# The joint output projection of a hybrid trunk layer: results kept in SBUF, norm and transposes at other places, and the order of five smaller steps

## The chip, the cores and the metric

The kernel runs on one core of one Trainium2 chip. The metric is device microseconds (us) of one execution; the time before is the median of three runs.

## The reference

One layer of a decoder, 2048 tokens of width 1024, all in float32:

```python
u    = rmsnorm(h, attn_pre_norm)
proj = u @ w_in                                     # 1024 -> 3584, split into:
hq, hf, hi, hg, sq, sk, sv = split(proj)            # 512 columns each
o_hg = rmsnorm(hgrn2_mix(hq, hf, hi), hg_out_norm) * silu(hg)   # recurrence, 4 heads of 128 x 128, chunks of 64
o_sb = rmsnorm(stick_breaking_mix(sq, sk, sv), sb_out_norm)     # causal attention, 8 heads of 64
mix  = concatenate([o_hg, o_sb]) @ w_out            # 1024 -> 1024
h    = h + rmsnorm(mix, attn_post_norm)
gate, up = split(rmsnorm(h, ffn_pre_norm) @ w_gate_up)          # 1024 -> 2 x 2816
h    = h + rmsnorm((silu(gate) * up) @ w_down, ffn_post_norm)
h    = h + (p @ ple_proj) * sigmoid(h @ ple_gate)
```

## The kernel before

The 2048 tokens are worked in four groups (0 to 3) of 512. A float32 operand is split into a high part, cast by ScalarE, and a low part, subtracted by VectorE or GpSimd (`split`, `w_prep`), and each product is three TensorE matmuls (`mm3`, L216 to L219: the lines of nearly all matmuls). A tile of 128 x 512 float32 has 256 KB. Results between the stages lie in HBM: `o_s` (raw results of recurrence and attention, eight tiles of each group, 0 to 3 of the recurrence and 4 to 7 of attention), `on_s` (the same normed), `un_s` (normed rows for the FFN), `u_s` (these rows transposed), `h_s` and `h2_s` (the residual stream).

TensorE's order is the program's order. The order of VectorE, ScalarE, GpSimd and SP (all DMAs are issued on SP's queue) is set by the framework's list scheduler from its own estimates, except for instructions put through `tc.keep_in_program_order`. Streams (Python generators) are laid between each other by `weave(main, slots, (stream, steps, phase), ...)`: so many slots of the main stream, with the steps of each other stream spread over them. A `Rate` gives a stream its share of steps per slot.

The stages in order of time:

- Input projection of the four groups (`in_proj`), with the attention (`att_stream`) and the recurrence (`hgrn`) woven in. `in_norm` norms the rows, `in_u` transposes them. The first projection's products use the PSUM banks of tag `mm`.
- `out_proj` of groups 0 and 1, 16 slots each. The rest of the attention is spread over 30 of the 32 slots (`2 * OP_SLOTS - 2`). In group 1's slots lie also `post_mix` of group 0 (`pm`: norm and residual, four tiles, written to `h_s` and `un_s`), the turn of these rows (`tu`), and `first_rows`, which prepares group 2's operands for the next stage.
- `out_pair`, the joint projection of groups 2 and 3 ("the pair"): seven block products in the order `CHAIN` (1, 2, 6, 3, 7, 5, 4), each of four steps of 12 matmuls. `w_prep` prepares the weights of the next product, `a_prep` its other operand; both come in the first two steps of a product. `scaled` multiplies a raw result by its row scales (`over_rows`) and stores it in `on_s`. `post_mix` and the turn of group 1 are woven in:

```python
weave(op, 2)
weave(op, 5, (pm, TT, 0))
weave(op, 5, (tu, 9, 0), (Stream(first_operands()), ND, 1))
```

- FFN (`gate_up`, `down`) and the gated embedding (`ple`), run by `Drive`. Its stage 0 begins with block products too, b0p1 and so on, whose operands are made by `t_first` (four tiles of a product) and `t_second`. Other work is hung on its steps by `at` and `spread`: `post_late` (norm and residual of groups 2 and 3) and `turner` (turn of these rows).

`turn` is used for all these transposes. It loads row tiles one pair of blocks ahead (`get`); for groups 2 and 3 ScalarE multiplies the loaded rows by `scales`. Then TensorE transposes four blocks of 128 x 128 into a bank, ScalarE evicts the bank into `e` and multiplies by the gain, and `e` is stored in `u_s`.

## Time and profile before

| | |
|---|---|
| median of three runs | 3021.26 us (3021.04 to 3026.05) |
| the profiled execution | 3015.62 us |
| its span | 3013.8 us |
| mean granted TensorE clock | 0.983 |
| TensorE busy | 2869.5 us |
| VectorE busy | 2105.5 us |
| ScalarE busy | 1575.3 us |
| GpSimd busy | 1425.1 us |

PE is TensorE's matmuls, PEld its weight loads, DVE is VectorE, ACT is ScalarE, POOL is GpSimd, and SPq is SP's queue of DMAs. A row of the waits such as `PE tr L914 <- DMA wr<-un_s: 21.8, 2, 13.8` reads: TensorE, about to write tile `tr` at line 914, waited for the DMA that fills `wr` from `un_s`; 21.8 us in all, 2 times, 13.8 us the longest. A row of the timeline gives the begin in us, the busy time of the group, the engine, line, operation, tiles and shapes, the count, and in brackets the idle time before it and what ended it. A row of the DMA list gives the count, the KB of each and the median us from issue to landing. The granted clock is the share of full speed that TensorE was given.

### The profile page before, as it was taken

The page shows a single profiled execution, that of the slowest core. Times are in us where ns is not written, and L with a number is a line of the kernel's source. Part 1 is how long each engine was busy: PE and PEld are TensorE (multiplying, and loading weights), DVE is VectorE, ACT ScalarE, POOL GpSimd, SP SyncE. Part 2 cuts the span into 40 slices and gives each one's busy share as a digit, 9 for nine tenths or more (in the row PEclk, how much of TensorE's full clock was granted, in tenths as well). Part 3 has the DMA queues.
Part 4 walks back from the last instruction along what each step waited for, and adds up shares of the span by engine and source line. Part 5 has one row for each costly group of instructions (what it writes and reads, how often), then busy time and mean ns, then how long its engine had stood idle before and what let it go on. Part 6 is the DMA issues. An engine that isn't in the chain of part 4 may idle for free. (4 is left out here: it accounts for less than half of the span.)

```text
span 3013.8 us, 51897 instructions
## 1 busy us (share of the span) xinstructions
PE 2869.5 (95%) x17772; PEld 2401.6 (80%) x17772; DVE 2105.5 (70%) x3035; ACT 1575.3 (52%) x3174; POOL 1425.1 (47%) x1412
## 2 busy tenths in 40 slices
PE   8899999999999999876889999999999999999999
PEld 7788788888887888865777777788888888888777
DVE  3766667687777777756877777755787766565685
ACT  5666766676767676754533334355533333445542
POOL 3344546555556667745443222255822121456653
PEclk9999999999999999987999999999999999999999
DMA  7975655565445454477876787777975555677975
GB/s 216 313 215 160 182 175 164 148 179 165 151 139 157 144 157 138 154 233 256 299 234 216 230 286 253 249 232 208 313 252 173 175 161 181 213 216 230 331 249 168
DMA packets 478712, 626.60 MB, mean 208 GB/s; under 512 B 44656, under 2 KB 270960, under 8 KB 478448
## 3 DMA queue, kind: packets, MB, share of 16 engines
q1 hardware_dynamic: 478448, 623.29, 65.8%
q8 instruction: 140, 2.29, 0.3%
q14 instruction: 124, 1.02, 0.1%
HBM read 455.88 MB, written 167.25 MB: 207 GB/s over the span
## 5 line engine op out<-in xcount | busy, mean ns | idle before, releaser
L980 POOL TENSOR_TENSOR wl<-wr,wh 128x512 fp32r<-128x512 f32 x256 | 375.2, 1473 | 437.4 <-ACT wh L979 390.3
L979 ACT CAST wh<-wr 128x512 fp32r<-128x512 f32 x600 | 350.7, 618 | 437.5 <-PE mm L218 91.2
L443 POOL TENSOR_TENSOR a<-be,ring 128x512 f32<-128x512 f32 (+2 forms) x320 | 321.7, 1005 | 405.2 <-DVE ring L439 372.8
L980 DVE TENSOR_TENSOR wl<-wr,wh 128x512 fp32r<-128x512 f32 x344 | 305.3, 895 | 179.2 <-ACT wh L979 154.5
L217 PE MATMUL mm<-uh,wh 128*128 128x512 f32 x992 | 412.1, 415 | 11.4 <-ACT uh L979 4.2
L219 PE MATMUL mm<-uh,wl 128*128 128x512 f32 x992 | 391.7, 395 | 6.2 <-DVE wl L980 6.1
L218 PE MATMUL mm<-ul,wh 128*128 128x512 f32 x992 | 391.3, 394 | 5.0 <-POOL ul L980 5.0
L439 DVE TENSOR_TENSOR_SCAN ring<-z,ring,be 128x512 f32<-128x512 f32 x192 | 245.6, 1279 | 95.1 <-ACT z L425 91.0
L217 PE MATMUL mm<-wh,uh 128*128 128x256 f32 (+1 forms) x856 | 266.7, 312 | 4.2 <-DVE vv L358 4.2
L218 PE MATMUL mm<-wl,uh 128*128 128x256 f32 (+1 forms) x856 | 252.6, 295 | 2.6 <-POOL wl L980 2.6
L219 PE MATMUL mm<-wh,ul 128*128 128x256 f32 (+1 forms) x856 | 252.2, 295 | 0.0
L217 PEld LDWEIGHTS mm<-uh,wh 128*128 128x128 f32 x992 | 188.5, 190 | 50.3 <-ACT uh L979 4.7
L219 PEld LDWEIGHTS mm<-uh,wl 128*128 128x128 f32 x992 | 188.1, 190 | 49.6 <-DVE wl L980 7.4
L456 DVE TENSOR_TENSOR al<-tr,ah 128x512 fp32r<-128x512 f32 (+1 forms) x320 | 191.7, 599 | 49.7 <-ACT ah L454 47.7
L424 ACT ACTIVATE be<-z 128x512 f32<-128x512 f32 (+2 forms) x320 | 171.1, 535 | 105.4 <-DVE z L422 65.9
L203 ACT CAST wh<-wr 128x512 fp32r<-128x512 f32 x256 | 158.7, 620 | 125.2 <-PE mm L218 65.2
L218 PEld LDWEIGHTS mm<-ul,wh 128*128 128x128 f32 x992 | 188.7, 190 | 37.2 <-POOL ul L980 5.5
L454 ACT CAST ah<-tr 128x512 fp32r<-128x512 f32 (+1 forms) x320 | 167.8, 524 | 81.2 <-PE tr L451 79.1
L204 POOL TENSOR_TENSOR wl<-wr,wh 128x512 fp32r<-128x512 f32 x128 | 168.6, 1317 | 81.7 <-ACT wh L203 75.3
L980 POOL TENSOR_TENSOR wl<-s,wh 128x512 fp32r<-128x512 f32 x44 | 67.9, 1547 | 259.2 <-ACT wh L979 232.5
L418 PE MATMUL z<-kt,q 128*128 128x512 f32 (+3 forms) x640 | 187.8, 374 | 0.0
L451 PE MATMUL tr<-ident,a 128*128 128x128 f32 x1088 | 175.8, 275 | 8.3 <-POOL a L443 8.0
(362 smaller groups left out, 7553.8 us busy)
## 6 DMA issues: line engine op xcount, KB each, us to landing
wr<-in_w_gate_up_dram SPq DMA_DIRECT2D x308, 256.0 KB, 4.0
wr<-in_w_in_dram SPq DMA_DIRECT2D x224, 256.0 KB, 3.2
wr<-hid_s SPq DMA_DIRECT2D x154, 256.0 KB, 3.3
wr<-in_w_down_dram SPq DMA_DIRECT2D x110, 256.0 KB, 3.8
wr<-h_s SPq DMA_DIRECT2D x96, 256.0 KB, 4.2
wr<-wd_s SPq DMA_DIRECT2D x88, 256.0 KB, 3.1
kt<-k_s SPq DMA_DIRECT2D x80, 256.0 KB, 3.2
vt<-v_s SPq DMA_DIRECT2D x80, 256.0 KB, 3.2
```

The lines of the kernel that those rows point to most:

```text
L204: (lo_engine or nc.gpsimd).tensor_tensor(lo, src, hi.bitcast(F32), op=ALU.subtract)
L217: nc.tensor.matmul(o, l[0], r[0], start=start, stop=False)
L218: nc.tensor.matmul(o, l[0], r[1], start=False, stop=False)
L219: nc.tensor.matmul(o, l[1], r[0], start=False, stop=stop)
L418: nc.tensor.matmul(z[:, :n], st["q"][i][:, tb * P:(tb + 1) * P], ch["k"][:, :n], start=i == 0, stop=i == 1)
L424: nc.scalar.activation(be[:, :n], z[:, :n], AF.Sigmoid, scale=0.125)
L439: nc.vector.tensor_tensor_scan(r[:, o:o + n][:, ::-1], z[:, :n][:, ::-1], be[:, :n][:, ::-1], init, op0=ALU.mult, op1=ALU.bypass)
L443: nc.gpsimd.tensor_tensor(a[:, :n], be[:, :n], r[:, o + 1:o + n + 1], op=ALU.mult)
L451: nc.tensor.transpose(tr[:, tb * P:(tb + 1) * P], ch["a"][tb][:, sb * P:(sb + 1) * P], ident)
L456: nc.vector.tensor_tensor(lo[:, lo_c:], tr[:, lo_c:], hi[:, lo_c:].bitcast(F32), op=ALU.subtract)
L979: nc.scalar.copy(hi, src)
L980: lo_engine.tensor_tensor(lo, src, hi.bitcast(F32), op=ALU.subtract)
```

## The change

Seven things are changed.

- First input projection: its products use two tags of banks (`mm`, `tr`: four banks) instead of one, and group 1's transposes use `z` in place of `tr`. The squares of `in_norm` for groups 2 and 3 are kept in program order.
- Attention is spread over 29 slots instead of 30 and drained after the thirteenth slot of group 1's projection. That projection is woven as 6 + 3 + 4 + 3 slots: `pm` of group 0 in the first 6, the turn from the tenth slot on. The last square of group 3's attention results is made there too, and both row scales of group 3 (`rr3`) are computed ahead of the pair.
- `out_pair` loads group 3's eight raw results into weight buffers (`wl`, `wh`, and two `wr`) and uses them from there; they are no longer stored in `on_s[3]` nor loaded from it. All are scaled at step 1 of the first product, where product 6's operands are made too, the low parts on VectorE. The weights of product 2 are prepared after these loads; the low parts of product 6's weights go to GpSimd.
- In the pair the norm of group 1 lies in slots 0 to 3, `first_operands` in slots 4 to 6, the turn in slots 7 to 11, and slot 12 holds the operands of the FFN's product 6 (`third_operands`), which were made in the FFN's first two steps.
- `t_second` of the FFN's first product goes one `k` to a step (steps 1 to 4) instead of two to a step (steps 2 and 3).
- In `turn` the multiplication by `scales` is taken out of the load and put behind the eviction of the second block, in program order.
- The turner of group 2 begins at step 34 instead of 36; both turners have one step more.

The diff; the changes of line numbers and of two signatures (`placed`, `rr`) are left out:

```diff
...
                     nc.vector.scalar_tensor_tensor(
                         shared, y, 1.0 / D, y, op0=ALU.mult, op1=ALU.mult, accum_out=ss[:, j:j + 1])
                 else:
-                    nc.scalar.activation(junk, y, AF.Square, scale=ROOT, accum_out=ss[:, j:j + 1])
+                    placed(nc.scalar.activation(junk, y, AF.Square, scale=ROOT, accum_out=ss[:, j:j + 1]))
         r = const.tile([P, 1], F32, tag="ssum", name="ssum", bufs=8)
         nc.gpsimd.tensor_scalar(r, ss[:, 0:1], ss[:, 1:2], EPS, op0=ALU.add, op1=ALU.add)
         if out is None:
...
             (nc.gpsimd if g == NG - 1 else nc.vector).tensor_tensor(raw, raw, r, op=ALU.mult)
         else:
             nc.vector.scalar_tensor_tensor(raw, raw, g_sb[:, i - HH:i - HH + 1], r, op0=ALU.mult, op1=ALU.mult)
-        nc.sync.dma_start(on_s[g][i], raw)
+        if g == NG - 2:
+            nc.sync.dma_start(on_s[g][i], raw)
 
     def first_rows(g, tt):
         acc = ev(name="oss")
...
                 if k % 2:
                     yield
 
-    def out_pair(g, tt, acc):
+    def out_pair(g, tt, rr):
         sw = {}
         cs = [{} for _ in range(TT)]
         raws, s2 = {}, {}
...
             else:
                 hi, lo = operand(wpool, "u", UB)
             nc.scalar.copy(hi, raw)
-            (V if k % 2 else G).tensor_tensor(lo, raw, hi.bitcast(F32), op=ALU.subtract)
+            (V if k % 2 and pos != 2 else G).tensor_tensor(lo, raw, hi.bitcast(F32), op=ALU.subtract)
             sw[prod, k] = hi, lo
 
         def a_prep(pos, k):
...
                 sub(V, s2[k], a12, s2[k])
                 t, e = s2[k], G
             elif prod == 7:
-                t, a21 = load(on_s[g][k]), load(on_s[g + 1][k])
-                sub(V, t, t, a21)
+                t = load(on_s[g][k])
+                sub(V, t, t, raws[k])
                 e = V
             elif prod == 5:
-                t, a22 = load(on_s[g + 1][k]), load(on_s[g + 1][HH + k])
-                add(V, t, t, a22)
+                t = raws[k]
+                add(V, t, t, raws[HH + k])
                 e = G
             else:
-                t, e = load(on_s[g + 1][HH + k]), V
+                t, e = raws[HH + k], V
             tt[prod, k] = split(wpool, "u", UB, t, e)
 
         def rows(half, j, i):
...
 
         def before(pos, i):
             if (pos, i) == (0, 1):
-                raws["r"] = [over_rows(row_scale(hgss[:, g + 1, :]), "tr", new_acc)]
+                raws["r"] = [over_rows(r, "tr", new_acc) for r in rr]
                 for k in range(HH):
                     scaled(g + 1, k, raws[k], raws["r"][0])
-            elif (pos, i) == (0, 3):
-                raws["ss"] = row_scale(tile_sums(acc))
-            elif (pos, i) == (1, 1):
-                raws["r"].append(over_rows(raws["ss"], "tr", new_acc))
                 for k in range(HH):
                     scaled(g + 1, HH + k, raws[HH + k], raws["r"][1])
                     t = load(on_s[g][k])
                     sub(V, t, raws[k], t)
                     add(V, t, t, raws[HH + k])
                     s2[k] = t
-                    tt[6, k] = split(wpool, "u", UB, t, G if k % 2 else V)
+                    tt[6, k] = split(wpool, "u", UB, t, V)
 
         def new_acc():
             return slot("acc", 0, "acc")
 
-        for pos in range(2):
-            for k in range(HH):
-                w_prep(pos, k)
-        for k in (*range(HH), *range(HH, ND)):
-            raws[k] = load(o_s[g + 1][k])
-        sq = new_acc()
-        nc.scalar.activation(sq, raws[ND - 1], AF.Square)
-        nc.gpsimd.tensor_tensor(acc, acc, sq, op=ALU.add)
+        for k in range(HH):
+            w_prep(0, k)
+        for i in range(ND):
+            if i in (2, 3):
+                raws[i] = slot("wr", 0, "wr")
+            else:
+                tag = "wh" if i % 2 else "wl"
+                raws[i] = wpool.tile([P, GT], F32, tag=tag, name=tag, bufs=3)
+            nc.sync.dma_start(raws[i], o_s[g + 1][i])
+        for k in range(HH):
+            w_prep(1, k)
         for pos, prod in enumerate(CHAIN):
             for i in range(TT):
                 before(pos, i)
...
                 r = new_in().rearrange("p (t d) -> p t d", t=2)
                 rows = src[2 * i * P:2 * (i + 1) * P, q * 256:(q + 1) * 256]
                 nc.sync.dma_start(r, rows.rearrange("(t p) d -> p t d", p=P))
-                for n in range(2):
-                    if scales:
-                        nc.scalar.activation(r[:, n, :], r[:, n, :], AF.Copy, scale=scales[2 * i + n])
-                    ts.append(r[:, n, :])
+                ts.extend((r[:, 0, :], r[:, 1, :]))
             return ts
+
+        def scale(ts):
+            if scales:
+                for t, r in zip(ts, scales):
+                    tc.keep_in_program_order(nc.scalar.activation(t, t, AF.Copy, scale=r))
 
         nxt = get(0)
         yield
+        if scales:
+            scale(nxt)
+            yield
         for q in range(4):
             ts = nxt
             nxt = get(q + 1) if q < 3 else None
...
                 else:
                     nc.scalar.activation(e, b, AF.Copy, scale=gain[:, k:k + 1])
                 nc.sync.dma_start(dst[k], e)
+                if nxt and c:
+                    scale(nxt)
                 yield
 
     def make_pt():
...
     for i in range(WARM):
         nc.tensor.transpose(warm[:, i % TT * P:(i % TT + 1) * P], ident, ident)
     Stream(in_u(in_norm(0), us[0], ["mm", "mm", "tr", "z", "z", "av", "tr", "hg"])).drain()
-    u1 = Stream(in_u(in_norm(1), us[1], ["z", "av", "tr", "hg"]))
+    u1 = Stream(in_u(in_norm(1), us[1], ["z", "av", "z", "hg"]))
     build_masks(nc, att, masks)
+    mm_tags[:] = ["mm", "tr"]
     main = Stream(in_proj(0, us[0], KQV))
     weave(main, ND // 2)
     later = tc.keep_in_program_order
...
     weave(main, ND, (u1, ND, 0))
     main.drain()
     u1.drain()
+    mm_tags[:] = ["mm"]
 
     units = [attention_steps(g) for g in range(NG)]
     res = [{} for _ in range(NG)]
...
             un.drain()
         main.drain()
     todo = total_units - spent + LAG + 2
-    rates = Rate(att_stream, 2, todo, 2 * OP_SLOTS - 2)
+    rates = Rate(att_stream, 2, todo, 2 * OP_SLOTS - 3)
     r2 = Rate(hgs[2], 1, HG_STEPS - 42, 2)
     r3 = Rate(hgs[3], 1, HG_STEPS, 2 * OP_SLOTS - 2)
     half = OP_SLOTS // 2
...
             weave(op, OP_SLOTS - 2, rates.part(OP_SLOTS - 2), r3.part(OP_SLOTS - 2))
         else:
             rows = Stream(first_rows(2, tto))
-            weave(op, half, rates.part(half), r3.part(half), (pm, TT, 0), (rows, 3, 1))
+            weave(op, 6, rates.part(6), r3.part(6), (pm, TT, 0), (rows, 3, 1))
+            weave(op, 3, rates.part(3), r3.part(3))
             tu = Stream(turn(un_s[0], u_s[0], g_ffn, ["tr"], xt, ev))
             acc3 = ev(name="oss")
             square_sums(acc3, 0, 3, range(HH - 1), xt)
-            weave(op, half, rates.part(half), r3.part(half), (tu, 9, 0), (rows, 6, 1))
+            weave(op, 4, rates.part(4), r3.part(4), (tu, 5, 0), (rows, 4, 1))
+            att_stream.drain()
+            square_sums(acc3, 0, 3, (HH - 1,), xt)
+            weave(op, 3, r3.part(3), (tu, 4, 0), (rows, 2, 1))
             hgs[3].drain()
-            att_stream.drain()
+            rr3 = [row_scale(hgss[:, 3, :]), row_scale(tile_sums(acc3))]
             rows.drain()
             side.close()
             big[0] = ctx.enter_context(tc.tile_pool(name="bigr", bufs=1, side="right"))
...
 
     drive = Drive([(gate_up(0, tt0), 3), (down(0), 4), (gate_up(1, tt1), 3), (down(1), 4),
                    (ple(0, ss0), 5), (ple(1, ss1), 5)])
-    op = Stream(out_pair(2, tto, acc3))
+    op = Stream(out_pair(2, tto, rr3))
     tu = Stream(turn(un_s[1], u_s[1], g_ffn, ["tr", "hg"], lambda: slot("wr", 0, "wr"), ev))
 
-    weave(op, 2)
-    weave(op, 5, (pm, TT, 0))
-    weave(op, 5, (tu, 9, 0), (Stream(first_operands()), ND, 1))
+    def third_operands():
+        for k in range(ND // 2):
+            t_first(0, tt0, 6, k)
+            yield
+
+    weave(op, 4, (pm, TT, 0))
+    weave(op, 3, (Stream(first_operands()), ND, 1))
+    weave(op, 5, (tu, 9, 0))
+    weave(op, 1, (Stream(third_operands()), ND // 2, 0))
     drive.prepare(2)
     op.drain()
     wpool_open.close()
...
         return turn(src, dst, gain, ["hg"], wr, acc, scales)
 
     for k in range(ND // 2):
-        at(0, k // 2, lambda k=k: t_first(0, tt0, 6, k))
-        at(0, 2 + k // 2, lambda k=k: t_second(0, tt0, k))
+        at(0, 1 + k, lambda k=k: t_second(0, tt0, k))
     spread(0, 6, post_late(NG - 2), 2 * TT, 3)
     spread(0, 19, post_late(NG - 1), 2 * TT, 4)
     for k in range(DFF // 256):
         at(0, 36 + 4 * k, lambda k=k: down_combos(k))
-    spread(0, 36, turner(h_s[2], u_s[2], g_ffn, rows_h[0]), 9, 2)
-    spread(0, 54, turner(h_s[3], u_s[3], g_ffn, rows_h[1]), 9, 2)
+    spread(0, 34, turner(h_s[2], u_s[2], g_ffn, rows_h[0]), 10, 2)
+    spread(0, 54, turner(h_s[3], u_s[3], g_ffn, rows_h[1]), 10, 2)
     spread(2, 59, make_pt(), 9, 2)
     for k in range(ND // 2):
         spread(1, 3 + 18 * k, t_all(1, tt1, k), 9, 2)
...
```

What the schedulers make of it, at three places.

VectorE in the pair, about the norm of group 1: `mix<-mix,rstd,gb` is the norm of a tile (the number tells the tile), `h<-h,mix` its residual, `cu` and `c_...` evictions of the pair's products, `ul<-wr,uh`, `wl<-wr,wh` low parts of operands. Before, the last two tiles:

```order
1447 L987 TENSOR_TENSOR c_18839<-z,cu 128x512
1448 L204 TENSOR_TENSOR ul<-wr,uh 128x512
1449 L864 SCALAR_TENSOR_TENSOR mix<-mix,rstd_18626,gb 128x512 x2
1450 L865 TENSOR_TENSOR h<-h,mix 128x512
1451 L864 SCALAR_TENSOR_TENSOR mix<-mix,rstd_18734,gb 128x512 x2
1452 L865 TENSOR_TENSOR h<-h,mix 128x512
1453 L980 TENSOR_TENSOR ul<-wr,uh 128x512 x2
1454 L987 TENSOR_TENSOR c_18900<-av,cu 128x512
```

And now, with the last tile:

```order
1445 L997 TENSOR_TENSOR cu<-av,cu 128x512
1446 L997 TENSOR_TENSOR cu<-mm,cu 128x512
1447 L778 TENSOR_TENSOR wl<-wr,wh 128x512
1448 L867 SCALAR_TENSOR_TENSOR mix<-mix,rstd_18613,gb 128x512 x2
1449 L990 TENSOR_TENSOR ul<-wr,uh 128x512
1450 L994 TENSOR_TENSOR wr<-wr,wl 128x512
1451 L994 TENSOR_TENSOR wr<-wr,wh 128x512
1452 L868 TENSOR_TENSOR h<-h,mix 128x512
1453 L997 TENSOR_TENSOR cu<-z,cu 128x512
```

The last tile's norm stood behind the third tile's at once; now two evictions and a low part of weights stand right ahead of it, and three other operations between it and its residual.

ScalarE in the FFN's stage 0, about a turner step: `acc<-hg` is the eviction of a transposed bank, `wr<-wr,row_scales` the scaling of loaded rows, `wh<-wr` casts of operands, `sg<-` the FFN's activation. Before:

```order
1904 L979 CAST wh<-wr 128x512 x4
1905 L919 ACTIVATE acc<-hg,g_ffn 128x512
1906 L979 CAST wh<-wr 128x512 x2
1907 L901 ACTIVATE wr<-wr,row_scales 128x256 x2
1908 L979 CAST wh<-wr 128x512
1909 L901 ACTIVATE wr<-wr,row_scales 128x256 x2
1910 L1164 ACTIVATE sg<-c_21541 128x512
1911 L919 ACTIVATE acc<-hg,g_ffn 128x512
```

And now:

```order
1905 L989 CAST wh<-wr 128x512 x4
1906 L927 ACTIVATE acc<-hg,g_ffn 128x512
1907 L989 CAST wh<-wr 128x512 x3
1908 L1174 ACTIVATE sg<-c_21502 128x512
1909 L927 ACTIVATE acc<-hg,g_ffn 128x512
1910 L908 ACTIVATE wr<-wr,row_scales 128x256 x4
1911 L989 CAST wh<-wr 128x512
```

The scaling of a load's rows stood between two evictions; now all four scalings stand behind the second eviction.

SP's queue of DMAs ahead of the pair: `o_s_7<-avo` stores the last attention result of group 3, `wr<-o_s_...` loads group 3's raw results, `un_s<-mix` stores normed rows of group 1, `wr<-wo_s` loads weights. Before:

```order
814 L866 DMA h_s_88<-h 128x512
815 L474 DMA o_s_7_152<-avo 64x512
816 L866 DMA h_s_88<-h 128x512
817 L964 DMA wr<-o_s_0_145 128x512
818 L964 DMA wr<-o_s_1_146 128x512
819 L964 DMA wr<-o_s_2_147 128x512
820 L964 DMA wr<-o_s_3_148 128x512
821 L964 DMA wr<-o_s_4_149 128x512
822 L964 DMA wr<-o_s_5_150 128x512
823 L964 DMA wr<-o_s_6_151 128x512
824 L964 DMA wr<-o_s_7_152 128x512
825 L870 DMA un_s_96<-mix 128x512 x2
```

And now, from the store of that result on (`xt<-o_s_7` is the load for its square, `xt<-un_s` loads rows of group 0 to be turned, `u_s<-ev` stores turned rows, `raw<-o_s` are loads of `first_rows`, `gb` and `h` loads of group 1's norm):

```order
804 L477 DMA o_s_7_152<-avo 64x512
805 L705 DMA xt<-o_s_7_152 128x512
806 L901 DMA xt<-un_s_95 128x2x256 x2
807 L928 DMA u_s_99<-ev 128x512 x2
808 L753 DMA raw<-o_s_6_143 128x512
809 L753 DMA raw<-o_s_7_144 128x512
810 L859 DMA gb<-in_attn_post_norm_dram 128x512 x2
```

The store stood just ahead of the eight loads of raw results; now the load for the last square follows it at once, and the loads into `wl` and `wh` come later (from row 813 on).

More of the change, by code (lines that the diff above doesn't have):

```diff
@@ L257, in dense_op, with row_rstd @@
             yield banks[i]
-    def row_rstd(halves, out=None, ss=None, shared=None):
+    def row_rstd(halves, out=None, ss=None, shared=None, placed=lambda ins: ins):
         if ss is None:
@@ L296, in in_norm @@
                     nc.sync.dma_start(halves[j], x[r0:r0 + P, j * GT:(j + 1) * GT])
-            r = row_rstd(halves, shared=att.tile([P, GT], F32, tag="be", name="sq") if g == 0 else None)
+            if g < 2:
+                r = row_rstd(halves, shared=att.tile([P, GT], F32, tag="be", name="sq") if g == 0 else None)
+            else:
+                r = row_rstd(halves, placed=tc.keep_in_program_order)
             for h in halves:
@@ L814, in before @@
                     s2[k] = t
-                    tt[6, k] = split(wpool, "u", UB, t, G if k % 2 else V)
+                    tt[6, k] = split(wpool, "u", UB, t, V)
         def new_acc():
             return slot("acc", 0, "acc")
-        for pos in range(2):
-            for k in range(HH):
-                w_prep(pos, k)
-        for k in (*range(HH), *range(HH, ND)):
-            raws[k] = load(o_s[g + 1][k])
-        sq = new_acc()
-        nc.scalar.activation(sq, raws[ND - 1], AF.Square)
-        nc.gpsimd.tensor_tensor(acc, acc, sq, op=ALU.add)
+        for k in range(HH):
[3 more added lines that the diff above has]
+                raws[i] = slot("wr", 0, "wr")
+            else:
+                tag = "wh" if i % 2 else "wl"
[3 more added lines that the diff above has]
+            w_prep(1, k)
         for pos, prod in enumerate(CHAIN):
```

## The prediction

> **What bounds the kernel now.** I read the page's slices first, then TensorE's waits, then the same stretches as windows, and last the timelines of the engines those waits name.
>
> ```profile
> span 3013.8 us, 51897 instructions
> PE 2869.5 (95%) x17772; PEld 2401.6 (80%) x17772; DVE 2105.5 (70%) x3035; ACT 1575.3 (52%) x3174; POOL 1425.1 (47%) x1412
> PE   8899999999999999876889999999999999999999
> PEclk9999999999999999987999999999999999999999
> ```
>
> TensorE is busy 95% of the span, so 3013.8 - 2869.5 = 144 us is all its idle time. Each digit is 75 us; the dip (7, 6, 8, 8 from slice 18 on) lies between 1280 and 1580 us, and there the granted clock drops too. Who ends the idle:
>
> ```profile
> PE tr L914 <- DMA wr<-un_s: 21.8, 2, 13.8
> PE hg L914 <- ACT acc L919: 11.6, 4, 3.7
> PE tr L914 <- DMA xt<-un_s: 8.3, 1, 8.3
> PE mm L219 <- DVE wl L980: 6.1, 1, 6.1
> PE tr L712 <- POOL oss L827: 5.4, 1, 5.4
> PE mm L218 <- POOL ul L980: 5.0, 1, 5.0
> PE mm L217 <- ACT uh L979: 4.2, 1, 4.2
> PE z L218 <- POOL ul L774: 3.1, 1, 3.1
> PE z L218 <- DVE ul L774: 1.9, 1, 1.9
> PE mm L217 <- ACT wh L979: 1.1, 1, 1.1
> PE mm L217 <- DVE vv L358: 4.6, 4, 1.5
> PE mm L217 <- DVE eb L344: 1.5, 2, 0.8
> ```
>
> Columns: total us, times, longest. The last two rows are those of the first 120 us. Windows (from:to, length, then busy time and count of PE, PEld, DVE, ACT and POOL, granted clock, DMA share, GB/s):
>
> ```profile
> 1205.60:1281.20 75.60, 67.67 (x720) 61.12 (x718) 57.64 (x86) 56.43 (x133) 57.46 (x70) 0.95 0.48 153
> 1290.10:1340.90 50.80, 45.17 (x488) 42.08 (x489) 31.93 (x49) 27.34 (x55) 25.01 (x24) 0.92 0.66 219
> 1339.00:1522.00 183.00, 133.80 (x561) 106.80 (x560) 130.46 (x168) 90.14 (x182) 94.14 (x80) 0.85 0.78 264
> 1424.00:1468.20 44.20, 43.73 (x207) 36.11 (x206) 32.96 (x45) 28.88 (x60) 24.11 (x26) 1.00 1.00 349
> 1468.20:1498.00 29.80, 29.24 (x129) 23.87 (x128) 27.67 (x43) 13.89 (x25) 8.58 (x7) 1.00 0.78 264
> 1523.00:1600.00 77.00, 77.00 (x341) 63.75 (x340) 58.42 (x82) 23.37 (x48) 27.02 (x22) 1.00 0.73 240
> 1700.00:1910.00 210.00, 198.40 (x889) 162.74 (x888) 153.94 (x229) 76.91 (x146) 46.00 (x33) 0.98 0.79 260
> ```
>
> The third, 1339 to 1522 us, is the joint projection of groups 2 and 3 ("the pair") and the start of the FFN up to the first rows of `post_late`: 49 us idle and a mean clock of 0.85. The change is aimed at this stretch and at four smaller places. I take them in order of time.
>
> **1. First input projection, four banks instead of two.** The `vv` and `eb` rows are TensorE waiting for a PSUM bank not yet evicted: 4.6 + 1.5 = 6.1 us. With four banks a whole group of products (48 matmuls of 77.00/341 = 0.226 us, 10.8 us) lies between two uses of a bank, against a longest wait of 1.5. The second group's transposes leave `tr` for `z`, so the banks do not collide. **-6.1** (0 to -6.1). The squares of `in_norm` for groups 2 and 3 are pinned to their place in ScalarE's order; no wait above names them: 0.
>
> **2. Turn of the first group's rows.** The 8.3 us wait is for the load of `un_s[0]`, whose last store comes just before it:
>
> ```profile
> 1282.73 0.94 SPq L870 DMA_DIRECT2D un_s<-mix  x2
> 1285.77 1.40 SPq L898 DMA_DIRECT2D xt<-un_s  x3
> un_s<-mix SPq DMA_DIRECT2D x16, 256.0 KB, 3.0
> xt<-un_s SPq DMA_DIRECT2D x8, 256.0 KB, 4.3
> ```
>
> Store and load land in 3.0 and 4.3 us. In the changed order the norm's last ScalarE row stands ahead of the copy `q<-hg` it stood behind, and TensorE's transposes one slot later (two steps of 12 short products with attention and recurrence between, some 5 us: 50.80 us over the last 8 slots less the waits). Together that covers 8.3. About 2 us of half clock go too: the second window has 0.92 over 50.8 us, a loss of 4, half of it after this wait. **-10.3** (-5 to -10.3).
>
> **3. Attention ends three slots before the pair.** The same attention now fills 13 slots of group 1's projection instead of 16, 23% more in each. GpSimd and VectorE, each busy 0.76 of the first window, take more there and less in the last three, where only the recurrence lies between the products. Its waits show what it costs when uncovered:
>
> ```profile
> PE hg L544 <- DVE ks L572: 4.1, 3, 3.1
> PE hg L533 <- DVE ks L572: 2.5, 1, 2.5
> PE hg L533 <- POOL qp L570: 2.2, 2, 1.8
> ```
>
> Three slots hold five steps of it. Bounds: if each waits 2 us (the rows' mean is 8.8/6 = 1.5), +10; if denser attention hides the earlier ones, -3. I take **+4**, near three waits of the mean. The last attention result now stands on SP as store and reload one behind the other; SP stops for the store's landing. Queued behind are two loads of turned rows and two of `first_rows`, used no sooner than the pair's fifth step; an `o_s` store lands in 2.8 us:
>
> ```profile
> o_s<-avo SPq DMA_DIRECT2D x32, 128.0 KB, 2.8
> ```
>
> So it is covered: 0, or 3 us were that slack gone.
>
> **4. The pair and the FFN's start.** Gone: 8 stores and 16 loads of 256 KB (one load is added), the square of the last result inside the pair, and with it the 5.4 us wait. Moved ahead: all eight results are loaded into weight buffers as these come free, both row scales are made before the first product, product 6's operands begin after step 0 instead of step 5 (the 3.1 and 1.9), and the second group's norm begins at slot 0 with three slots between its end and the transposes (the 21.8). Product 6's FFN operands (12 loads, 12 VectorE operations, 4 casts) go into the pair's last slot, and `t_second` is dealt one `k` a step (the 6.1, 5.0, 4.2 and 1.1). All of these together are 48.6 us, and the half clock behind them as much again as a third.
>
> But nearly the same VectorE and GpSimd work must then fit in less time. Between the same marks (second group's first norm operation to `post_late`'s first) VectorE has 168 instructions before and 163 after, GpSimd 46 large ones and 45. TensorE's own floor: 561 matmuls at 44.20/207 = 0.2135 us make 120 us. VectorE's: 130.46/168 = 0.777 us each, times 163 = 127 us. VectorE, not TensorE, limits the stretch, and it is never full: 32.96/44.20 = 0.75, 27.67/29.80 = 0.93, 58.42/77.00 = 0.76 in the windows. At 0.93 the stretch is 136 us; at 0.76 it is 167. I take 0.88, nearer to 0.93, since that is the row in which it worked off a backlog, as it will: 127/0.88 = 144. **-39** (-16 to -63). Late next is the norm's last tile. Before:
>
> ```profile
> 1409.91 1.42 DVE L864 SCALAR_TENSOR_TENSOR mix<-mix,rstd,gb 128x512 f32<-128x512 f32 x2 [4.49 <-POOL rstd L272]
> 1420.77 0.69 PE L914 MATMUL tr<-ident,wr 128*128 128x128 f32 x2 [13.82 <-DMA wr<-un_s]
> ```
>
> 10.9 us from this operation to the transposes. In the changed order it stands behind the eviction of step 10, and TensorE has steps 11 to 13 (36 matmuls, 8.2 us) until it turns: some 3 to 8 us of the 21.8 stay, and they are in the 144.
>
> How crowded VectorE can get, the timeline shows:
>
> ```profile
> 1355.09 5.87 POOL L732 TENSOR_TENSOR wr<-wr,acc 128x512 f32<-128x512 f32 x4
> 1358.06 5.74 DVE L984 TENSOR_TENSOR wr<-wr 128x512 f32<-128x512 f32 x4
> 1510.74 1.28 DVE L984 TENSOR_TENSOR wr<-wr 128x512 f32<-128x512 f32 x2
> 1353.87 1.26 POOL L827 TENSOR_TENSOR oss<-oss,acc 128x512 f32<-128x512 f32 x1 [5.89 <-DMA un_s<-mix]
> ```
>
> The same subtraction takes 0.64 us alone and 1.44 beside GpSimd. [...]
>
> **5. FFN turns.** ScalarE scales rows as soon as they are asked for and stands in front of the eviction:
>
> ```profile
> 1726.69 0.91 ACT L901 ACTIVATE wr<-wr,row_scales 128x256 f32<-128x256 f32 x2 [16.74 <-DMA wr<-h_s]
> 1729.34 0.67 ACT L919 ACTIVATE acc<-hg,g_ffn 128x512 f32<-128x512 f32 x1
> 1730.06 0.66 PE L914 MATMUL hg<-ident,wr 128*128 128x128 f32 x4 [3.74 <-ACT acc L919]
> ```
>
> Now the scaling comes after the eviction of the second transposed block, two hooks after the load's issue. The 11.6 us go; the scaling itself (same count) has two FFN steps of slack. Of half clock the last window loses 0.02 x 210 = 4 us; I count 0.4. **-12** (-6 to -15).
>
> **Sum:** -6.1 - 10.3 + 4 - 39 - 12 = -63.4. The profiled execution took 3015.62 us (span 3013.8 and 1.8 around it), 5.6 below the median of 3021.26; I subtract from the median, as that is compared: **2958 us**. About 0.2%, 6 us, is what can be told from no change.
>
> **Rivals.**
> A, the two engines block each other fully: 163 x 0.64 + 45 x 1.26 = 161 us for the stretch, -22 instead of -39: 2975. For it: the rows above. [...] Chance 0.16.
> B, the 21.8 us wait stays whole, as the norm's chain crosses VectorE, GpSimd, ScalarE and SP, each with a queue: 16 us lost of the 39, 2974. For it: the 4.49 us that VectorE waited for `rstd`. Against: the norm starts two slots sooner. Chance 0.08.
> C, TensorE is the limit everywhere: -63 in the stretch, -3 in term 3, the rest as above: 2931 at a sum of -90. Against: the 127 us. Chance 0.07.
> D, slower: every VectorE operation in the stretch takes the crowded 1.44 us: 163 x 1.44 = 235, +52 there, 27 with the others: 3048. It decides from 183 + 24.4 = 207 us on, that is 1.27 us an operation against 0.777. Chance 0.04.
> E, the change moves waits without shortening: attention packed into 13 slots makes group 1's projection wait as long as the rest gains. It would need 57 us in 13 slots that now have some 9 us of such waits. Chance 0.04 (within 0.2%).
>
> **How the numbers follow.** Forecast 0.61, by itself 2944 to 2972 (terms' inner bounds). The range, 2938 to 2990, takes in A, B and nearly the two together (2975 + 16 = 2991), and leaves out C, D and E: 0.15. Faster 0.92 (forecast, A, B, C), same 0.04 (E), slower 0.04 (D).
>
> **What would show it.** Right: no TensorE wait for `vv` in the first 120 us; none for `xt<-un_s`; none for `oss`; `wr<-un_s` under 8 us; no wait of the `hg` transposes for the eviction in the FFN; the stretch 140 to 150 us with VectorE at 0.85 or more of it; recurrence waits some 4 us up. Wrong: the stretch over 160 us with VectorE operations above 0.9 us in the mean (A); a long `un_s` wait (B); TensorE or SP held behind loads into weight buffers; or waits in the middle of the FFN's first stage that were not there before.

## The result and the profile after

The changed kernel takes 2986.02 us (median of four runs, 2981.62 to 2990.73), the kernel before 3021.15: a ratio of 0.9884, 95% interval 0.9861 to 0.9907, or 35 us less. The forecast was 2958 and a range of 2938 to 2990. A second measurement, beside other kernels, gave 2988.97 and 0.9887 (0.9868 to 0.9906).

The page of the changed kernel (span, busy time, two rows of the slices):

```profile
span 2988.8 us, 51860 instructions
PE 2873.0 (96%) x17772; PEld 2402.3 (80%) x17772; DVE 2106.8 (70%) x3035; ACT 1575.5 (53%) x3174; POOL 1432.1 (48%) x1412
PE   8999999999999999887899999999999999999999
PEclk9999999999999999998999999999999999999999
```

TensorE's idle time fell from 144 to 2988.8 - 2873.0 = 116 us. The dip in the middle is narrower, but still there. Those of TensorE's waits of after, over the whole span, that bear on the terms (total us, times, longest):

```profile
PE tr L922 <- DMA wr<-un_s: 8.2, 1, 8.2
PE mm L217 <- ACT uh L989: 6.0, 1, 6.0
PE mm L218 <- DVE wl L778: 5.5, 1, 5.5
PE mm L217 <- DVE vv L361: 5.4, 4, 3.6
PE z L217 <- ACT wh L989: 5.4, 3, 3.2
PE hg L922 <- ACT wr L908: 4.8, 2, 2.8
PE z L218 <- POOL ul L778: 3.2, 2, 2.4
```

Gone are the 8.3 us for `xt<-un_s`, the 5.4 for `oss` and the 11.6 for the eviction `acc`. The `un_s` wait fell from 21.8 to 8.2. In exchange, rows stand here that were not there before: a low part of the pair's weights (`wl` at L778), and the scaled rows themselves in the FFN turns (`wr` at L908). The low parts `ul` of the pair's weights, 3.2 us here, stood at 5.0 before (3.1 and 1.9, then at L774).

The next table cuts the profiled executions at five marks: the attention's first product, the first VectorE accumulation of group 1's output projection, the first matmul of the pair, the first turned block of the FFN, the first product of the down stage. The columns are the lengths between them, in us, and the last one of the table is the ratio of all runs to before. For example the pair and the FFN's start, in the changed kernel, lie between these two rows of TensorE's timeline:

```profile
1325.58 0.47 PE L217 MATMUL mm<-uh 128*128 128x512 f32 x1
...
1676.38 0.60 PE L922 MATMUL hg<-ident,wr 128*128 128x128 f32 x4
```

| kernel | start | projections | group 1's output projection | pair and FFN's start | FFN turns | ratio to before (95%) |
|---|---|---|---|---|---|---|
| before | 96.2 | 1152.5 | 92.2 | 362.5 | 230.1 | 1 |
| changed | 91.5 | 1152.7 | 81.4 | 350.8 | 225.5 | 0.9884 (0.9861 to 0.9907) |
| changed, again | 91.6 | 1156.7 | 81.6 | 349.4 | 226.9 | 0.9887 (0.9868 to 0.9906) |
| banks_old | 100.7 | 1150.8 | 81.8 | 348.6 | 228.2 | 0.9915 (0.9900 to 0.9930) |
| att_old | 92.7 | 1156.0 | 90.8 | 346.8 | 228.4 | 0.9903 (0.9886 to 0.9921) |
| weave_old | 92.4 | 1152.7 | 82.5 | 356.3 | 226.5 | 0.9911 (0.9896 to 0.9926) |
| raws_old | 91.7 | 1152.1 | 81.6 | 361.0 | 227.4 | 0.9918 (0.9903 to 0.9932) |
| turner_old | 91.5 | 1154.6 | 83.3 | 347.5 | 231.9 | 0.9882 (0.9864 to 0.9900) |
| combos_late | 91.1 | 1152.4 | 82.7 | 349.0 | 214.5 | 0.9943 (0.9928 to 0.9958) |
| lows_v | 90.6 | 1152.2 | 81.4 | 341.9 | 225.1 | 0.9851 (0.9829 to 0.9874) |
| v_turn_later | 91.3 | 1152.9 | 81.8 | 347.0 | 227.1 | 0.9858 (0.9841 to 0.9875) |
| v_turn_sums | 92.1 | 1152.0 | 82.5 | 348.4 | 224.2 | 0.9876 (0.9854 to 0.9897) |
| v_combos | 91.6 | 1154.6 | 81.8 | 342.2 | 222.2 | 0.9820 (0.9804 to 0.9835) |

The profiled execution of before took 5.5 us less than its median, that of the changed kernel 4.7 more, so the two differ by 25 us where the medians differ by 35. From the start to the down stage the five columns gain 4.7 - 0.2 + 10.8 + 11.7 + 4.6 = 31.6 us; behind that the changed kernel's profile is 6.6 us the longer one, and its repetition 0.5.

A stage that a kernel shares with the changed one agrees with it within 2 us (start, output projection) to 4 us (the two last columns); only the long projections spread over 6. So a stage of one profile can show an effect of 5 us, which the time of a whole run, with its interval of 5 to 7 us to either side, can't.

### The profile page after: what moved, and what is told of

It reads as the page before. It is cut to its first block, busy times and chain, and to the rows that moved or that the text cites. A ratio compares the mean times of both kernels' runs of the same rounds, so it can differ in the third digit from the quotient of the medians.

```text
span 2988.8 us, 51860 instructions
## 1 busy us (share of the span) xinstructions
PE 2873.0 (96%) x17772; PEld 2402.3 (80%) x17772; DVE 2106.8 (70%) x3035; ACT 1575.5 (53%) x3174; POOL 1432.1 (48%) x1412
## 4 chain that ended last, share of the span: by engine, by line
PE 41%; DMA 5%; issue 5%; DVE 4%; POOL 3%; ACT 1%; SPq 0%; POOLq 0%; DVEq 0%; ACTq 0%
PE mm L217 4%; PE mm L218 4%; PE mm L219 4%; PE z L219 4%; PE z L218 4%; PE z L217 4%; PE tr L219 3%; PE tr L217 3%; PE tr L218 3%; PE av L217 2%; PE av L219 2%; PE av L218 2%; DMA wr<-in_w_gate_up_dram 1%; DVE wr L994 1%; POOL wl L990 1%
## 5 line engine op out<-in xcount | busy, mean ns | idle before, releaser
L990 POOL TENSOR_TENSOR wl<-wr,wh 128x512 fp32r<-128x512 f32 x256 | 366.3, 1438 | 428.5 <-ACT wh L989 392.3
L217 PE MATMUL mm<-uh,wh 128*128 128x512 f32 x960 | 397.3, 414 | 11.0 <-ACT uh L989 6.0
L218 PE MATMUL mm<-ul,wh 128*128 128x512 f32 x960 | 377.5, 393 | 0.8 <-POOL ul L990 0.8
L219 PE MATMUL mm<-uh,wl 128*128 128x512 f32 x960 | 377.6, 393 | 0.1
L442 DVE TENSOR_TENSOR_SCAN ring<-z,ring,be 128x512 f32<-128x512 f32 x192 | 245.6, 1279 | 100.7 <-ACT z L428 95.9
L217 PE MATMUL mm<-wh,uh 128*128 128x256 f32 (+1 forms) x824 | 256.2, 311 | 1.4 <-DVE vv L361 1.3
L218 PE MATMUL mm<-wl,uh 128*128 128x256 f32 (+1 forms) x824 | 244.1, 296 | 9.9 <-DVE wl L778 5.5
L219 PE MATMUL mm<-wh,ul 128*128 128x256 f32 (+1 forms) x824 | 243.2, 295 | 0.0
L219 PEld LDWEIGHTS mm<-uh,wl 128*128 128x128 f32 x960 | 181.0, 189 | 41.0 <-DVE wl L990 0.5
L204 POOL TENSOR_TENSOR wl<-wr,wh 128x512 fp32r<-128x512 f32 x128 | 168.5, 1317 | 85.2 <-ACT wh L203 73.8
L218 PEld LDWEIGHTS mm<-ul,wh 128*128 128x128 f32 x960 | 182.0, 190 | 31.9 <-POOL ul L990 1.4
L990 POOL TENSOR_TENSOR wl<-s,wh 128x512 fp32r<-128x512 f32 x44 | 74.7, 1701 | 266.5 <-ACT wh L989 209.0
```

The costliest lines, as they stand in the source:

```text
L204: (lo_engine or nc.gpsimd).tensor_tensor(lo, src, hi.bitcast(F32), op=ALU.subtract)
L217: nc.tensor.matmul(o, l[0], r[0], start=start, stop=False)
L218: nc.tensor.matmul(o, l[0], r[1], start=False, stop=False)
L219: nc.tensor.matmul(o, l[1], r[0], start=False, stop=stop)
L442: nc.vector.tensor_tensor_scan(r[:, o:o + n][:, ::-1], z[:, :n][:, ::-1], be[:, :n][:, ::-1], init, op0=ALU.mult, op1=ALU.bypass)
L990: lo_engine.tensor_tensor(lo, src, hi.bitcast(F32), op=ALU.subtract)
```

## The experiments

The first four, lows_v to weave_old, ask where term 4's missing 25 us went. Then att_old and banks_old undo terms 3 and 1, turner_old and combos_late ask after term 5, and last come versions that follow from the answers. No run undoes the pinning of the squares in `in_norm` by itself.

**lows_v.** The low parts of the pair and of `t_second`, and one scaling, on VectorE:

```diff
-            (V if k % 2 and pos != 2 else G).tensor_tensor(lo, raw, ...)
+            V.tensor_tensor(lo, raw, ...)
-                t, e = s2[k], G                      # product 3; product 5 likewise
+                t, e = s2[k], V
-            (nc.gpsimd if g == NG - 1 else nc.vector).tensor_tensor(raw, raw, r, ...)
+            nc.vector.tensor_tensor(raw, raw, r, ...)
-        tt[3, k] = pair_of(b22, "u", 3, G)           # product 5 likewise
+        tt[3, k] = pair_of(b22, "u", 3, V)
```

> Changed kernel, with all low parts of the pair and of t_second, and the scaling of the fourth group's first four results, on VectorE instead of partly on GpSimd (30 operations of 256 KB). Theory 1, the two engines exclude each other on SBUF: a pair of operations takes 1.7 us side by side (0.6 + 1.1) and 1.2 us on VectorE alone, so the stretch from the second group's first norm operation to the first of post_late goes from 168 us to about 150, VectorE operations there from a mean near 0.89 us to under 0.75, and the time from 2986 to about 2970. Theory 2, VectorE is simply full and GpSimd relieves it: 30 x 0.6 = 18 us more on VectorE, the stretch goes to 178 to 186 us and the time to about 3000.

The stretch between the two norm marks as windows, of the changed kernel and of lows_v (from:to, length, busy time and count of PE, PEld, DVE, ACT and POOL, clock, DMA share, GB/s):

```profile
1328.20:1496.30 168.10, 131.73 (x527) 102.55 (x526) 133.29 (x163) 87.95 (x180) 96.08 (x78) 0.87 0.73 250
```

```profile
1325.90:1483.10 157.20, 134.12 (x545) 105.95 (x544) 126.28 (x197) 87.63 (x180) 48.59 (x43) 0.89 0.79 269
```

VectorE did 34 operations more in 7 us less: its mean fell from 133.29/163 = 0.82 to 126.28/197 = 0.64 us (the expectation's 0.89 was too high), and the stretch by 10.9, or by 8 against the changed kernel's repetition (165.2). Operand splits of both, grouped by line (busy us, mean ns, then idle time ahead), first the changed kernel's, with one operation of VectorE that reads a PSUM bank in the third row:

```profile
L204 DVE TENSOR_TENSOR ul<-wr,uh 128x512 fp32r<-128x512 f32 x8 | 11.4, 1447 | 0.0
L778 POOL TENSOR_TENSOR ul<-wr,uh 128x512 fp32r<-128x512 f32 x8 | 12.1, 1517 | 11.2 <-ACT uh L777 10.6 <-DMA un_s<-mix 0.7
L997 DVE TENSOR_TENSOR c<-mm,cu 128x512 f32<-128x512 f32 x7 | 4.8, 681 | 0.1
```

```profile
L204 DVE TENSOR_TENSOR ul<-wr,uh 128x512 fp32r<-128x512 f32 x14 | 9.9, 733 | 0.0
L778 DVE TENSOR_TENSOR ul<-wr,uh 128x512 fp32r<-128x512 f32 x12 | 8.1, 684 | 4.6 <-ACT uh L777 4.6
```

Theory 1 holds in its times: subtractions side by side took some 1.5 us each in the mean (1447 and 1517 ns), and one after the other on VectorE 0.7 each (733 and 684 ns). An operation of the same size with one input in PSUM took 0.68 us (681 ns) in the changed kernel too, so it is not VectorE as a whole that was slower. That the two engines exclude each other was the author's explanation: the rows show how long the operations took beside each other (1447 ns against 733), not why. The size was about half of what was expected (157 us, not 150), since other waits then ended last: `un_s` 4.6, `ul` 4.6 and the FFN's operands. The whole time was 2979.07 us, between the theories (2970 and 3000) and 7 to 10 below the changed kernel's two medians; the intervals of the ratios overlap a little, so the stretch shows more than the time.

**turn_other.** `turn(un_s[1], ...)` reads `un_s[0]` instead.

> Changed kernel, but the turn in the pair reads the first group's rows, which were stored long before, instead of the second group's (its output is another for that reason; all instructions stay). It prices the wait for un_s (8.2 us in one piece, with 6.8 us of half clock behind it). Theory 1: the wait and the half clock are lost time: the stretch goes from 168 to about 157 us. Theory 2: TensorE runs into the next operands (the products' own low parts are as late): the wait reappears under another name within the next 20 us, and the stretch stays at 165 or more.

The `un_s` wait is gone, and in this single run the pair and FFN's start take 344.9 us against 346.8 to 350.8 (mean 348.7) in the six kernels with the same pair: some 4 us, hardly beyond their spread. Between the norm marks it is 162.6 us, where theory 1 had 157 and theory 2 at least 165. The wait and what its half clock cost behind it would be 10: of the 6.8 us at half that the expectation counts, 3.3 lie inside the wait (see the last section), and 3.5 us at half (0.50) lose 1.75. A part came back: a wait of 2.7 us at an FFN operand that the changed kernel does not have. The truth lay between the theories.

How little one wait says of a stage, att_old (below) shows. In its pair this wait is 20.2 us, and the stage is the shortest of the six with 346.8: TensorE is idle there for 39.3 us in all, against 38.5 in the changed kernel.

```profile
PE tr L922 <- DMA wr<-un_s: 20.2, 1, 20.2
```

**raws_old.** The results stored in `on_s[3]` and loaded again, through the buffers of `load`, and the weights of product 2 prepared ahead of these loads as before:

```diff
-            raws[i] = (tiles of wl, wh; two wr)      # used from SBUF
+            raws[i] = load(o_s[g + 1][i])            # scaled, stored in on_s
-                sub(V, t, t, raws[k])                # products 5 and 4 likewise
+                sub(V, t, t, load(on_s[g + 1][k]))
```

> Changed kernel, but the fourth group's normed results stored to HBM and loaded again, as before (8 stores and 16 loads of 256 KB more, one load less). Theory 1, these transfers were hidden (DMA share 0.75 in the stretch) and keeping the results in SBUF moved nothing: within 3 us. Theory 2, SP's queue stops for slots and landings (20.8 us of waits on VectorE in the stretch already): the pair is 6 to 12 us longer.

Theory 2: the pair took 361.0 us, some 12 more. The `un_s` wait nearly doubled, and SP's timeline shows why: the loads of the turn's rows stood behind four loads of weights that took 9.8 us, 8.1 of them waits for low parts of weights (`ul` at L777) on VectorE and GpSimd. The third fence has the same place in the changed kernel, three loads in 3.0 us. That the stores and loads of the results alone did this is not shown, since the order of the weights changed with them.

```profile
PE tr L915 <- DMA wr<-un_s: 15.2, 1, 15.2
```

```profile
1390.13 9.77 SPq L771 DMA_DIRECT2D wr<-wo_s  x4
1399.99 2.43 SPq L894 DMA_DIRECT2D wr<-un_s  x5
```

```profile
1391.68 3.02 SPq L772 DMA_DIRECT2D wr<-wo_s  x3
1394.79 2.43 SPq L901 DMA_DIRECT2D wr<-un_s  x5
```

**weave_old.** The slots and hooks of before for norm, turn, `first_operands`, product 6's operands and `t_second` (the three `weave` lines quoted above).

> Changed kernel with the norm, the turn and the FFN's first operands at the slots of before (norm from slot 2 over 5, turn and first operands together over the last 5, product 6's operands and t_second in the FFN's first steps). Theory 1, these positions are what shortened the pair and the FFN's start (from 362.5 us, first matmul of the pair to the first turned block of the FFN, to 350.8): it goes back to 360 to 365, with un_s waits of some 20 us. Theory 2, the stretch is bound by what VectorE and GpSimd do in it, wherever it stands: 350 to 355.

356.3 us, 7 more than the changed kernel's mean of 349, with 22.2 us of waits for `un_s`. Both theories are half right. Undoing the positions costs 7 us of the stage's gain of 13.5, undoing the results kept in SBUF 12: together more than the gain, so the two overlap.

**att_old.**

```diff
-    rates = Rate(att_stream, 2, todo, 2 * OP_SLOTS - 3)
+    rates = Rate(att_stream, 2, todo, 2 * OP_SLOTS - 2)
...
-            att_stream.drain()
-            square_sums(acc3, 0, 3, (HH - 1,), xt)
-            weave(op, 3, r3.part(3), (tu, 4, 0), (rows, 2, 1))
+            weave(op, 3, rates.part(3), r3.part(3), (tu, 4, 0), (rows, 2, 1))
+            att_stream.drain()
+            square_sums(acc3, 0, 3, (HH - 1,), xt)
```

> Changed kernel, but attention spread over 30 slots as before and drained ahead of the pair; the last square and the second row scale come behind it, still ahead of the pair. Theory 1, ending the attention early is worth it, since the last result's store, load, square and row sums (3 + 4 us of landing, then three engines) no longer stand before the pair: TensorE reaches the pair's second step 5 to 10 us later than the changed kernel does. Theory 2, the prediction's term 3 (packing costs about 4 us): it reaches the pair's first step 3 to 5 us sooner and loses nothing behind.

Theory 1: 90.8 us to the pair instead of 81.4, of which 6.7 are the row sums of the last result:

```profile
1337.74 1.87 PE L715 MATMUL tr<-ones,oss 128*128 128x1 f32 x8 [6.68 <-POOL oss L710]
```

Without these, 2.7 us more, not 4 less, where the stage spreads over 2. So the packing costs nothing that can be seen. Why the rest is a little shorter is not shown.

**banks_old.** `mm_tags` and the tags of the second group's transposes as before.

> Changed kernel with one tag of banks for the first input projection's products and the second group's transposes, as before. By the prediction's term the small waits for vv and eb come back (6.1 us) and the attention's first product, at 91.5 us in the changed kernel and 96.2 before, starts at 96 to 97 us. Rival, by the changed trace, in which two new waits of 3.3 and 3.6 us stand in their place: the start moves by less than 2 us.

The start took 100.7 us, 9 more than in the changed kernel: the term holds, the rival does not. The size is less sure, since before, with the same banks, took 96.2. TensorE's idle time up to this mark is 12.4 us here, 11.3 before and 8.4 in the changed kernel; the other 5 of the 9 us are busy time, at a lower granted clock (0.94 from 21 us on, against 0.98 in the changed kernel and 1.00 before).

**turner_old.** The scaling back in `get`, first turner at step 36.

> Changed kernel with the FFN's turn as before (scaling at the load, first turner at step 36). By the prediction's term the turn's waits go from 4.8 back to 11.6 and the time up by 12 us (2998). By the trace, in which two of the four waits stayed, about 2 x 2.7 to 6.8 us of waits plus some half clock: up by 5 to 8 us (2992). A rival, that the turners do not matter since other waits take their place: within 3 us.

The stage took 231.9 us against 225.5 to 228.4 (mean 227.2) in the six kernels with the new turner and the same FFN: 5 us by the trace's reading, not the term's 12; the whole time (2989.14) can't tell it from the changed kernel. Why two waits stayed, ScalarE's timeline of the changed kernel shows, with TensorE's next transposes under it:

```profile
1682.28 0.63 ACT L989 CAST wh<-wr 128x512 fp32r<-128x512 f32 x1 [0.69 <-PE mm L218]
1699.91 0.62 ACT L989 CAST wh<-wr 128x512 fp32r<-128x512 f32 x1 [17.01 <-DVE wr L994]
1700.97 0.67 ACT L927 ACTIVATE acc<-hg,g_ffn 128x512 f32<-128x512 f32 x1
1701.54 1.69 ACT L908 ACTIVATE wr<-wr,row_scales 128x256 f32<-128x256 f32 x4
1702.09 0.33 PE L922 MATMUL hg<-ident,wr 128*128 128x128 f32 x1 [2.81 <-ACT wr L908]
```

A cast of product 6's weights held ScalarE for 17 us, and eviction and scaling behind it. It waited for VectorE's combination of six loads of `w_gate_up`, which SP issued late, behind the loads and stores of `down_combos` (SP's timeline, and under it VectorE's):

```profile
1682.22 1.71 SPq L974 DMA_DIRECT2D wr<-in_w_down_dram  x2
1687.01 1.05 SPq L1012 DMA_DIRECT2D wd_s<-wr  x2
...
1690.30 3.11 SPq L974 DMA_DIRECT2D wr<-in_w_gate_up_dram  x6
```

```profile
1696.65 0.69 DVE L997 TENSOR_TENSOR s<-wr 128x512 f32<-128x512 f32 x1 [5.16 <-DMA wr<-in_w_gate_up_dram]
```

**combos_late.** `at(0, 36 + 4 * k, ...)` for `down_combos` becomes `at(1, k, ...)`.

> Changed kernel with the eleven down_combos moved from FFN stage 0 (beside the turners) to the first steps of stage 1. Theory: the two turn waits that are left (2.8 and 2.0 us) come from a cast that held ScalarE 17 us, waiting for weight loads which stood behind the loads and stores of down_combos in SP's queue; without them the turn waits go under 1 us in all and the time falls by 5 to 8 us (2980). Rival: the work only moves, and stage 1 waits for VectorE or for wd_s instead: 2986 to 2995, with new TensorE waits between 1950 and 2050 us.

TensorE has no wait at all in the turns, and the stage falls to 214.5 us: that `down_combos` beside the turners cause the waits is shown. That they do so by SP's queue, and not by their work on VectorE, only the timelines above say, since the edit moves both. But the rival is right on the time, 3007.34 us, and beyond its bounds: stage 1 waits for casts instead, and from the down stage's first product to TensorE's last one it takes 1114.4 us against 1081.9.

```profile
PE mm L217 <- ACT wh L989: 9.7, 3, 4.4
PE z L217 <- ACT wh L989: 7.8, 2, 6.3
```

**v_turn_later** is lows_v with `first_operands` over four slots instead of three, so that the turn comes one slot later.

> lows_v with the turn and the slot of product 6's FFN operands one slot (two steps) later. Theory: the wait for un_s that lows_v still has (4.6 us and 6.8 us of half clock) is covered by two steps, the stretch from the pair's first matmul to the FFN's first turned block goes from 341.9 us to about 335, and the time falls by 6 more (lows_v had 2979). Rival: the later turn makes the FFN's product 6 wait for u_s (its loads stand on SP behind stores that have not landed): a new wait of 4 to 8 us between 1440 and 1460 us, and no gain.

The rival: no `un_s` wait, but a larger one at the FFN's first products, in a stage of 347.0 us against lows_v's 341.9, and a whole time no better (2980.25 us against 2979.07).

```profile
1436.14 0.79 PE L217 MATMUL tr<-uh,wh 128*128 128x512 f32 x1 [7.48 <-ACT wh L989]
```

**v_turn_sums** adds `tile_sums(acc3)` and its row scale one slot earlier.

> v_turn_later with the row sums of the fourth group's attention results and their row scale one slot earlier, in the last slots of group 1's projection. Theory: the wait of the pair's second step for the row scale (2.9 us in lows_v, with some half clock) goes, 3 to 5 us less than v_turn_later. Rival: GpSimd, which makes the scale, is held there by low parts of weights either way, and the wait stays or moves to the first scaled result: within 2 us.

The 3.9 us wait for `rq` went, but the stage took 348.4 us, no less: the wait at the FFN's operand had grown to 9.8 us. The rival was right on the time, though the wait moved elsewhere than it said.

**v_combos** is lows_v with

```diff
-        at(0, 36 + 4 * k, lambda k=k: down_combos(k))
+        at(0, 36 + 7 * (k // 2) + k % 2, lambda k=k: down_combos(k))
```

> lows_v with the eleven down_combos still in FFN stage 0, but two by two in the steps of each block in which no weights are loaded (products 7 and 5 are then prepared; steps 36, 37, 43, 44 and so on to 71, instead of every fourth step from 36). Theory: the cast that holds ScalarE 17 us waits for product 6's six loads of weights, which meet the loads and stores of down_combos on SP; apart from each other, the turn waits that lows_v has (2.4 and 3.3 us) go, and TensorE reaches the down stage 5 to 10 us sooner than in lows_v (from the first turned block 220 instead of 225.1 us); the time 2970 to 2976. Rival: two at once crowd SP and the load buffers more than one by itself, and the waits grow: 2980 or more.

2970.66 us (2963.39 to 2973.94), a ratio of 0.9820 (0.9804 to 0.9835): the best version, 15 us under the changed kernel, whose interval lies apart from this one. In its turns ScalarE's casts wait less for VectorE's combinations and more for the loads themselves (the first two rows are lows_v's, the others this version's, all of 1660 to 1900 us), but the longest single wait falls from 16.6 to 9.7 us. TensorE's waits for scaled rows fall from lows_v's 5.7 to 3.8 us; the stage is 2.9 us shorter, less than the 5 expected. Of the 8 us by which the median is under that of lows_v, the rest is not explained, and the two intervals overlap a little.

```profile
ACT wh L989 <- DVE wr L994: 38.2, 5, 16.6
ACT wh L989 <- DMA wr<-in_w_gate_up_dram: 3.9, 2, 3.1
```

```profile
ACT wh L989 <- DMA wr<-in_w_gate_up_dram: 27.0, 8, 9.7
ACT wh L989 <- DVE wr L994: 16.5, 5, 8.4
```

## Why the prediction was right, and where it was wrong

The direction, four of the five terms' signs and the range were right; the gain was 35 us instead of 63. The forecast's own band, 2944 to 2972, was missed: 2986 lies in the part of the range that was there for rivals A and B, 4 us from its end, and one of the four runs (2990.73) lies beyond it. Rival C's sum is added up wrongly: its terms make -94.4, not -90, and 2927 us.

- **Term 1 (-6.1): right.** 91.5 us instead of 96.2, and 100.7 in banks_old: 5 to 9. The prediction said that no `vv` wait would be left in the first 120 us; one of 3.6 us is, behind the attention's first product, and the wait for `ul` grew from 1.7 to 3.3.
- **Term 2 (-10.3): right**, within what can be told from term 3. The wait went (0.7 left).
- **Term 3 (+4): wrong in its sign.** The two together are 92.2 - 81.4 = -10.8, where -6.3 was forecast. The failed step is the price put on the denser attention, three waits of 1.5 us: att_old, without the packing, is 2.7 us longer and not 4 shorter once its row sums are taken off.
- **Term 4 (-39): wrong in its size.** It came out at 362.5 - 349 = -13 (-15 between the norm marks: 183 to 168). The failed step is "I take 0.88, nearer to 0.93": VectorE was busy 133.29/168.10 = 0.79, and the operations got slower as they were packed, 0.82 us in the mean instead of the 0.777 taken over. Of the 24 us between 144 and 168 the share makes 17 and the mean 7 (133.29/0.88 = 151, where 127/0.88 = 144 was forecast). Rival A, 161 us for the stretch at a chance of 0.16, was nearer, and lows_v shows that VectorE's operations were slower beside GpSimd's (0.82 us in the mean against 0.64), which makes 8 to 11 us of the 24; that the two block each other fully is not shown. What held VectorE's share at 0.79 is not shown; in lows_v it is 126.28/157.20 = 0.80. The mean of before, 0.777, said nothing against A, since it belonged to a stretch with GpSimd less often beside VectorE (busy 94.14/183.00 = 0.51 of it, and 96.08/168.10 = 0.57 after). Two of the waits taken as gone (3.1 and 1.9) were put down to product 6's operands; their rows name L774, the low parts of its weights, and 3.2 of these 5.0 us stayed. The others came half back: in the FFN's start 6.0 and 3.2 us of the 16.4, and for the pair's weights the 5.5, where VectorE's subtraction stood behind the norm's last tile and its neighbours:

```profile
1376.85 0.69 DVE L778 TENSOR_TENSOR wl<-wr,wh 128x512 fp32r<-128x512 f32 x1 [0.23 <-ACT wh L777]
1377.99 2.44 DVE L867 SCALAR_TENSOR_TENSOR mix<-mix,rstd,gb 128x512 f32<-128x512 f32 x2 [0.46 <-POOL rstd L272]
1380.35 0.68 DVE L990 TENSOR_TENSOR ul<-wr,uh 128x512 fp32r<-128x512 f32 x1
1380.95 1.75 DVE L994 TENSOR_TENSOR wr<-wr,wl 128x512 f32<-128x512 f32 x1
...
1385.03 0.68 DVE L778 TENSOR_TENSOR wl<-wr,wh 128x512 fp32r<-128x512 f32 x1
```

- **The `un_s` wait** ("some 3 to 8 us stay"): 8.2, at the edge. Rival B did not come.
- **Term 5 (-12): half.** About 3 to 5: 230.1 and 231.9 with the old turner, 227 in the mean with the new one. The failed step is "two FFN steps of slack": ScalarE worked its instructions in the order given, and a cast ahead of the scaling held it for 17 us, more than that.
- The prediction named what would show it wrong: the stretch over 160 us with slower VectorE operations. That is what the windows show, though the mean stayed under the 0.9 us that it gave.

## What to carry to other kernels

Price a stretch by the slowest engine's work only after asking what each operation costs beside the neighbour that it will then have; a mean from a looser schedule was too cheap here (0.777 us an operation before, 0.82 after). Where VectorE and GpSimd share out operations on SBUF and VectorE is the bound, giving more of them to VectorE can be the faster split (0.64 against 0.82 us an operation here, and 8 to 11 us of the stretch). Where one queue is worked in order, putting the operation that suffers at another place took away half of the wait here (11.6 to 4.8 us); the rest hung on a cast that waited 17 us, and went only when the work that delayed its loads was moved. A wait that is taken away shows its worth only after the next in line is known (turn_other 4 of 10 us, v_turn_later none).

## What the runs showed of the hardware

A wait cost more than its length here. In the 8.2 us wait for `un_s` of the changed kernel (1390.96 to 1399.11) the granted clock was 1.00 up to 1395 us and half (0.50) from 1396 on, and it stayed at half for 3.5 us behind the wait, as windows before, behind and after its end show:

```profile
1395.80:1399.10 3.30, 0.00 (x0) 0.00 (x0) 3.30 (x3) 0.00 (x0) 3.30 (x3) 0.50 0.88 290
1399.10:1402.60 3.50, 3.49 (x10) 2.81 (x11) 1.78 (x2) 0.69 (x1) 1.24 (x1) 0.50 1.03 350
1402.60:1406.00 3.40, 3.40 (x16) 2.81 (x15) 0.69 (x1) 1.24 (x2) 0.62 (x1) 0.99 0.43 150
```

10 matmuls ran in the second window and 16 in the third, of nearly the same length. In the third the clock was back at 0.99.
